# A hybrid decoder layer on one core: the selection of one token block beside the scatter of another

## The chip, the cores and the metric

The kernel runs on one core of one Trainium2 chip. The time is that of one execution on the device, in microseconds (us). A core has five engines with queues of their own: TensorE (PE, with its weight loads shown as PEld), VectorE (DVE), ScalarE (ACT), GpSimd (POOL) and SyncE (SP, which here issues transfers). Each works through its instructions in the order that the program gives, and waits on semaphores for the others.

## The reference

One layer of a causal decoder for 512 tokens of width 1024: latent attention and a convolution beside each other, then a retrieval over experts (PEER), then a gate and a norm. The change lies in the retrieval:

```
q = (xb @ w_q).reshape(P, 8, 2, 64)
s = einsum('phcd,hcnd->phcn', q, sub_keys)            # 8 heads x 2 halves x 128 keys
v1, i1 = top_k(s[:, :, 0], 16); v2, i2 = top_k(s[:, :, 1], 16)
cand = v1[..., :, None] + v2[..., None, :]            # 256 sums for each head
best, pos = top_k(cand, 16)
g = softmax(best)
act = gelu(xb . u_tab[e]);  out = sum over h,k of g * act * v_tab[e]
```

There are 128 x 128 experts; each token picks 8 x 16 of them.

## The kernel before

**Dense and gathered tokens.** The 512 tokens are four blocks of 128. Block 0 gathers its experts' rows from `u_tab` and `v_tab` by indirect transfers (POOL issues them, DVE multiplies: `gu`, `gj`, `gv`, `acc`). Blocks 1 to 3 are computed densely: for each of 128 expert tiles e (128 experts each) `dense_act(e)` multiplies the tile of `u_t` by the 384 tokens in 24 matmuls (`aps`, each fp32 product as three matmuls of split halves, lines 149 to 151) and applies Gelu (`act`); later `dense_out(e)` multiplies by the gates and by the tile of `v_tab` in 18 matmuls (`vps`). Every tile is loaded (`tr`), split into a high half on ACT (`th`, L136) and a low half on DVE (`tl`, L141), two units ahead of its use.

**The early stage.** Before the first `dense_out`, the gates of blocks 1 to 3 must lie in DRAM as a table `gd`. So a first stage runs EARLY = 65 of the tiles' `dense_act` and beside them, on the other engines, the routing. `topk(t)` is called for blocks 0, 1, 2, 3 in turn and has two parts. *Selection*, on DVE: 16 rows of keys (five operations each, two of them with a value load ahead: `tv`, `ti`, `sc`; half of the rows of blocks 0 and 1 lie ahead of this stage), eight heads of candidates (five operations each: `bv`, `bp`, `cand`), softmax and the decoding of the picks (`ge`, `oh`, `sel` and others). For block 0 it ends in `pidx`, with which the gathers can start. *Scatter*, for blocks 1 to 3: three transposes on PE (`str`, L916 to L918) bring picks and gates into another layout, ACT copies them (`ids`, `gsc`), and then 16 groups of eight tokens follow. A group is one comparison on DVE (`o12`, 2048 elements, shown in rows of the trace as `o`), two multiplications by the high and the low part of the gate (`og`, 1024 elements each, L945), 16 matmuls on PE (`gp`, L962 and L963) and two evictions on ACT (`stg`, L964); after two groups SP stores 1 MB to `gd` (L967).

**What sets the order.** The loop over the tiles hands out the routing in small steps: each `yield` in `topk` names its cost on DVE and PE, and steps are taken while the DVE's sum is below a pace times the PE's sum. The kernel's recording layer then schedules: it simulates the engines by its own costs and may move instructions past each other within an engine where nothing depends on them. The gathers of block 0 (18 in this stage) are spread over the tiles from G_FROM on.

**Storage.** Scores (`sc`) of the four blocks share one pool of four buffers with the staging of the scatter (`stg`). Gelu results wait in a ring of RING = 17 buffers; EARLY - RING = 48 of them are spilled to DRAM and loaded back later.

**The end of the stage.** `load_gates` (L1014) reads the first part of `gd` back (`gch`) once the last `stg` has been stored; `prep_out` multiplies it by `act` (`cf`, L1027), splits that (`ch`, `cl`), and the first `vps` can run. After that, `dense_act` and `dense_out` alternate, tile by tile.

Of the kernel before, what the change touches and what calls it, by code (L numbers as in the profile page):

```python
# [46 lines left out]
RING = 17  # L47
# [4 lines left out]
EARLY = 65  # L52
# [6 lines left out]
G_FROM = 20  # L59
EARLY_TOP = (0, 1)  # L60
TOP_PACE = 4
ROUTE_V = 237.0
# [3 lines left out]
A_M = 3.9  # L66
# [28 lines left out]
def hymba_layer(ctx, tc, x, xT, p_t, pos, pvec, conv_ln_g, conv_ln_b, w_in, w_uq, w_ukv, w_out,  # L95
# [52 lines left out]
    def mm3(ps, lh, ll, rh, rl, first, last):  # L148
        nc.tensor.matmul(ps, lh, rh, start=first, stop=False)  # L149
        nc.tensor.matmul(ps, lh, rl, start=False, stop=False)  # L150
        nc.tensor.matmul(ps, ll, rh, start=False, stop=last)  # L151
# [549 lines left out]
    s8p = s8.enter_context(tc.tile_pool(name="s8p", bufs=4, side="right"))  # L701
    sc = [s8p.tile([P, 2 * NH, NK], F32, name=f"sc{t}", tag="s8") for t in range(NT)]
# [7 lines left out]
    with ExitStack() as fs:  # L710
# [3 lines left out]
        def best_keys(t, rs):  # L714
            if t not in tops:
                new_top(t)
            s, (tv, ti) = sc[t], tops[t]
            for r in rs:
                h, c = divmod(r, 2)
                nc.vector.max(out=tv[:, h, c, 0:8], in_=s[:, r])  # L720
                nc.vector.max_index(out=ti[:, h, c, 0:8], in_max=tv[:, h, c, 0:8], in_values=s[:, r])
                nc.vector.match_replace(out=s[:, r], in_to_replace=tv[:, h, c, 0:8], in_values=s[:, r],
                                        imm_value=-3e38)
                nc.vector.max(out=tv[:, h, c, 8:16], in_=s[:, r])
                nc.vector.max_index(out=ti[:, h, c, 8:16], in_max=tv[:, h, c, 8:16], in_values=s[:, r])
                yield 1.0, 0.0
# [42 lines left out]
    ready = {}  # L769

# [13 lines left out]
    def dense_act(e):  # L784
        hi, lo = ready.pop(("A", e))
        ps = ps_a.tile([P, TD], F32, name="aps", tag="a")
        for k in range(KD):
            mm3(ps, hi[:, k], lo[:, k], xnh[:, k, P:], xnl[:, k, P:], k == 0, k == KD - 1)
# [31 lines left out]
    with ExitStack() as fs:  # L820
# [14 lines left out]
        def topk(t):  # L835
# [12 lines left out]
            for h in range(NH):  # L848
# [6 lines left out]
                yield (1.9 if h == 0 else 0.8), 0.0  # L855
# [37 lines left out]
            for j0, w in ((0, 8), (8, 16)):  # L893
# [6 lines left out]
                yield (1.2 if w == 16 else 0.7) + (1.8 if j0 == 0 else 0.0), 0.0  # L900
# [3 lines left out]
                yield (1.2 if w == 16 else 0.7), 0.0  # L904
# [5 lines left out]
                yield (0.9 if j0 == 0 else 1.4), 0.0  # L910
            if t == 0:
                nc.vector.scalar_tensor_tensor(pidx, sel[:, 0], float(NK), sel[:, 1], op0=ALU.mult, op1=ALU.add)
                return
# [3 lines left out]
            nc.tensor.transpose(pt[:, 1], sel[:, 1], identf)  # L917
            nc.tensor.transpose(pt[:, 2], pg, identf)  # L918
            ids = ohp.tile([P, P // PAIR, 2, PAIR], F16, name="ids", tag="ids")
            nc.scalar.activation(ids, pt[:, 0:2].rearrange("p c (g q) -> p g c q", q=PAIR), AF.Copy)  # L920
            gh = ohp.tile([P, P], F16, name="gh", tag="gh")
            gl = ohp.tile([P, P], F16, name="gl", tag="gl")
            gs = ohp.tile([P, P], F32, name="gsc", tag="gsc")
            nc.scalar.activation(gs, pt[:, 2], AF.Copy, scale=GSC)
            nc.vector.tensor_copy(gh, gs)
            nc.vector.tensor_tensor(gl, gs, gh, op=ALU.subtract)
            yield 1.2, 0.3

            late = []
            for c in range(P // TCH):  # L930
                stg = s8p.tile([P, NK, TCH], F32, name="stg", tag="s8")
                for c0 in range(0, TCH, OCH):
                    cs = slice(c * TCH + c0, c * TCH + c0 + OCH)
                    ng = OCH // PAIR
                    gs0 = cs.start // PAIR
                    o12 = ohp.tile([P, ng, 2, NK, PAIR], F16, name="o12", tag="o12")
                    og = ohp.tile([P, 2, ng, NK, PAIR], F16, name="og", tag="og")
# [3 lines left out]
                        ids[:, gs0:gs0 + ng].rearrange("p g c q -> p (g c) q").unsqueeze(2)  # L941
                        .to_broadcast([P, 2 * ng, NK, PAIR]), op=ALU.is_equal)
                    yield 1.2, 0.0
# [5 lines left out]
                    o1 = o12[:, :, 0]  # L949
                    late.append((c, c0, stg, o1, og))  # L950
                    if len(late) > LATE:
                        scatter(t, *late.pop(0))
                    yield 1.1, 0.94
# [3 lines left out]
        def scatter(t, c, c0, stg, o1, og):  # L957
            for q in range(0, OCH, 4):
                gp = ps_g.tile([P, 4, NK], F32, name="gp", tag="gp")
                for i in range(4):  # L960
                    g, r = divmod(q + i, PAIR)
                    nc.tensor.matmul(gp[:, i], o1[:, g, :, r], og[:, 0, g, :, r], start=True, stop=False)  # L962
                    nc.tensor.matmul(gp[:, i], o1[:, g, :, r], og[:, 1, g, :, r], start=False, stop=True)  # L963
# [4 lines left out]

        def route():
            for t in (0, 1, 2, 3):  # L970
                yield from topk(t)
# [7 lines left out]
        for e in range(EARLY):  # L979
# [5 lines left out]
            while ngat < want:  # L985
# [3 lines left out]
            while vec < pace * mat:  # L989
                v, m = next(rt, (1e9, 0.0))  # L990
                vec += v
                mat += m
        for _ in rt:
            pass
# [255 lines left out]
```

## Time and profile before

| | us |
|---|---|
| median of 3 runs | 1554.48 (1546.46 to 1557.81) |
| profiled execution, its own time | 1550.69 |
| its span, first to last instruction | 1548.7 |
| PE busy | 1490.1 (96%) |
| DVE busy | 1263.9 (82%) |
| ACT busy | 715.5 (46%) |

The mean granted clock of TensorE is 0.99 of its full level. A matmul's duration overlaps that of the next one, so the busy time of PE is read together with counts: how many matmuls end in a stretch. The same holds on DVE, where the next instruction starts a little before the end of the one ahead; so costs are taken from start to start. The stage that the change touches lies between the first `aps` at 331.8 us and the first `vps` at 684.6 us of the span.

### The profile page before, as it was taken

The page shows a single profiled execution, that of the slowest core. Times are in us where ns is not written, and L with a number is a line of the kernel's source. Part 1 is how long each engine was busy: PE and PEld are TensorE (multiplying, and loading weights), DVE is VectorE, ACT ScalarE, POOL GpSimd, SP SyncE. Part 2 cuts the span into 40 slices and gives each one's busy share as a digit, 9 for nine tenths or more (in the row PEclk, how much of TensorE's full clock was granted, in tenths as well). Part 3 has the DMA queues.
Part 4 walks back from the last instruction along what each step waited for, and adds up shares of the span by engine and source line. Part 5 has one row for each costly group of instructions (what it writes and reads, how often), then busy time and mean ns, then how long its engine had stood idle before and what let it go on. Part 6 is the DMA issues. An engine that isn't in the chain of part 4 may idle for free.

```text
span 1548.7 us, 22818 instructions
## 1 busy us (share of the span) xinstructions
PE 1490.1 (96%) x8070; PEld 1314.2 (85%) x8070; DVE 1263.9 (82%) x2614; ACT 715.5 (46%) x1160; POOL 414.6 (27%) x302
## 2 busy tenths in 40 slices
PE   8999989999899998999999999999999999999997
PEld 6888878799798998899999898888999888878876
DVE  6999665699999999968868777697978788778766
ACT  7468864444484753843333323232333343333444
POOL 0000010001001010014545454364545345435000
PEclk9999989999999999999999999999999999999999
DMA  7321124526587775799999898889999999999642
GB/s 229 103 83 55 49 76 162 177 79 207 170 304 228 260 271 198 269 328 351 336 316 333 304 342 307 307 318 329 341 325 340 336 336 344 342 353 315 225 141 95
DMA packets 167682, 386.55 MB, mean 250 GB/s; under 512 B 13328, under 2 KB 82320, under 8 KB 164496
## 3 DMA queue, kind: packets, MB, share of 16 engines
q1 hardware_dynamic: 130128, 249.82, 47.2%
q0 software_dynamic: 36864, 134.23, 24.1%
q8 instruction: 63, 1.03, 0.3%
q10 hardware_dynamic: 576, 1.05, 0.2%
q14 instruction: 51, 0.42, 0.1%
HBM read 343.63 MB, written 41.42 MB: 249 GB/s over the span
## 4 chain that ended last, share of the span: by engine, by line
DMA 20%; issue 15%; PE 10%; DVE 6%; POOL 5%; ACT 2%; SPq 0%; POOLq 0%; DVEq 0%; ACTq 0%
DMA gu<-in_u_tab,pidx 8%; DMA gv<-in_v_tab,pidx 7%; PE vps L150 3%; PE vps L151 3%; PE vps L149 3%; DMA tr<-in_v_tab 3%; POOL gv L814 3%; POOL gu L803 2%; DMA tr<-in_u_t 1%; DVE tl L141 1%; DVE gj L807 1%; DVE acc L817 1%; DVE cf L1027 1%; ACT th L136 1%; DVE cl L141 1%
## 5 line engine op out<-in xcount | busy, mean ns | idle before, releaser
L136 ACT ACTIVATE th<-tr 128x1024 fp32r<-128x1024 f32 x256 | 270.8, 1059 | 554.9 <-DMA tr<-in_u_t 269.2
L141 DVE SCALAR_TENSOR_TENSOR tl<-tr,th 128x1024 fp32r<-128x1024 f32 x256 | 312.1, 1219 | 119.4 <-ACT th L136 118.9
L149 PE MATMUL aps<-mixh,th 128*128 128x384 f32 x1024 | 348.8, 341 | 4.4 <-ACT act L790 4.4
L151 PE MATMUL aps<-mixh,tl 128*128 128x384 f32 x1024 | 347.5, 339 | 1.1 <-DVE tl L141 1.0
L150 PE MATMUL aps<-mixl,th 128*128 128x384 f32 x1024 | 346.7, 339 | 0.0
L803 POOL DMA_INDIRECT gu<-in_u_tab,pidx x128 | 176.6, 1380 | 533.9 <-DVE gj L807 357.7
L150 PE MATMUL vps<-tl,ch 128*128 128x512 f32 x768 | 301.1, 392 | 7.3 <-DVE tl L141 7.3
L149 PE MATMUL vps<-th,ch 128*128 128x512 f32 x768 | 299.2, 390 | 1.7 <-ACT th L136 1.7
L151 PE MATMUL vps<-th,cl 128*128 128x512 f32 x768 | 299.9, 391 | 0.0
L814 POOL DMA_INDIRECT gv<-in_v_tab,pidx x128 | 211.5, 1653 | 237.0 <-DVE acc L817 201.1
L149 PEld LDWEIGHTS aps<-mixh,th 128*128 128x128 f32 x1024 | 193.9, 189 | 9.0 <-ACT act L790 6.7
L151 PEld LDWEIGHTS aps<-mixh,tl 128*128 128x128 f32 x1024 | 193.8, 189 | 2.7 <-DVE tl L141 2.7
L150 PEld LDWEIGHTS aps<-mixl,th 128*128 128x128 f32 x1024 | 194.0, 189 | 2.3
L807 DVE SCALAR_TENSOR_TENSOR gj<-gu,xn 128x1024 bf16<-128x1024 f32 x128 | 156.1, 1220 | 33.2 <-DMA gu<-in_u_tab,pidx 32.1
L150 PEld LDWEIGHTS vps<-tl,ch 128*128 128x128 f32 x768 | 144.1, 188 | 40.3 <-DVE tl L141 11.8
L817 DVE SCALAR_TENSOR_TENSOR acc<-gv,gact,acc 128x1024 f32<-128x1024 f32 x128 | 163.8, 1279 | 16.8 <-DMA gv<-in_v_tab,pidx 16.0
L149 PEld LDWEIGHTS vps<-th,ch 128*128 128x128 f32 x768 | 144.2, 188 | 31.1 <-ACT th L136 2.5
L151 PEld LDWEIGHTS vps<-th,cl 128*128 128x128 f32 x768 | 144.1, 188 | 29.8
L964 ACT ACTIVATE stg<-gp 128x512 f32<-128x512 f32 x96 | 94.8, 1110 | 21.4 <-PE gp L963 13.7
L136 ACT ACTIVATE ch<-cf 128x384 fp32r<-128x384 f32 x128 | 66.2, 519 | 72.4 <-DVE cf L1027 45.0
L138 ACT ACTIVATE wh<-wr,pv 128x512 fp32r<-128x512 f32 (+2 forms) x84 | 55.1, 694 | 53.2 <-PE bank L151 25.8
L141 DVE SCALAR_TENSOR_TENSOR cl<-cf,ch 128x384 fp32r<-128x384 f32 x128 | 70.5, 551 | 8.2 <-ACT ch L136 8.2
(301 smaller groups left out, 2178.1 us busy)
## 6 DMA issues: line engine op xcount, KB each, us to landing
tr<-in_u_t SPq DMA_DIRECT2D x128, 512.0 KB, 5.7
tr<-in_v_tab SPq DMA_DIRECT2D x128, 512.0 KB, 6.8
gd<-stg SPq DMA_DIRECT2D x24, 1024.0 KB, 4.9
gch<-gd SPq DMA_DIRECT2D x64, 384.0 KB, 10.2
ad<-act SPq DMA_DIRECT2D x48, 192.0 KB, 4.0
aback<-ad SPq DMA_DIRECT2D x48, 192.0 KB, 6.8
wr<-in_gate_w SPq DMA_DIRECT2D x12, 512.0 KB, 3.3
wr<-in_w_out SPq DMA_DIRECT2D x8, 512.0 KB, 3.3
```

The costliest lines, as they stand in the source:

```text
L136: nc.scalar.activation(hi, src, AF.Copy)
L138: nc.scalar.activation(hi, src, AF.Copy, scale=g)
L141: nc.vector.scalar_tensor_tensor(lo, src, 1.0 if g is None else g, hi.bitcast(F32), op0=ALU.mult, op1=ALU.subtract)
L149: nc.tensor.matmul(ps, lh, rh, start=first, stop=False)
L150: nc.tensor.matmul(ps, lh, rl, start=False, stop=False)
L151: nc.tensor.matmul(ps, ll, rh, start=False, stop=last)
L803: nc.gpsimd.indirect_dma_start(out=g, out_offset=None, in_=u_tab, in_offset=bass.IndirectOffsetOnAxis(ap=pidx[:, s:s + 1], axis=0))
L807: nc.vector.scalar_tensor_tensor(junk, g, 1.0, xn0, op0=ALU.mult, op1=ALU.mult, accum_out=gact[:, s:s + 1]))
L814: nc.gpsimd.indirect_dma_start(out=g, out_offset=None, in_=v_tab, in_offset=bass.IndirectOffsetOnAxis(ap=pidx[:, s:s + 1], axis=0))
L817: nc.vector.scalar_tensor_tensor(acc0, g, gact[:, s:s + 1], acc0, op0=ALU.mult, op1=ALU.add))
L964: nc.scalar.activation(stg[:, :, c0 + q:c0 + q + 4].rearrange("p n t -> p t n"), gp, AF.Copy, scale=1.0 / GSC)
L1027: nc.vector.tensor_tensor(cf.rearrange("p (c t) -> p c t", t=TCH), a.rearrange("p (c t) -> p c t", t=TCH), gch[c][:, :, e % GCH], op=ALU.mult)
```

## The change

1. *Selection and scatter become separate functions.* `topk(t)` is split into `select(t)` and `gates(t, slots)`. The order of the blocks was selection 0, selection and scatter 1, selection and scatter 2, selection and scatter 3. It becomes: selection 1; the scatter of 1 beside selection 0 and then selection 2; the scatter of 2 beside selection 3; the scatter of 3. `side_by_side` deals the steps of two generators in proportion.
2. *The transposes wait for tiles.* `gates` yields nothing until two further expert tiles have been handed out, then issues its three transposes behind the last matmul of the newest tile (`issue_after`), and splits the gates on DVE one tile later.
3. *One multiplication for a group's gates.* High and low part of the gate lie in one tile `ghl`; the group's two multiplications of 1024 elements become one of 2048, with four free dimensions.
4. *Storage and numbers.* Each score block has a buffer of its own, and a scatter stages in the buffers that are free by then. RING is 18, EARLY 66 (so 48 tiles are spilled as before), the 18 early gathers begin at tile 41 instead of 21 and not before `pidx` is there, and the costs in the `yield`s and of the pace are new.

```diff
-RING = 17
+RING = 18
-EARLY = 65
+EARLY = 66
-G_FROM = 20
+G_FROM = 40
-ROUTE_V = 237.0
+ROUTE_V = 255.0
-A_M = 3.9
+A_M = 4.16
...
+        def tiles_later(n):
+
+            e = last_tile[0] + n
+            while last_tile[0] < e:
+                yield None
+
+        def gates(t, slots):
+            yield from tiles_later(2)
+            sel, pg = chosen.pop(t)
 
             pt = ps_tr.tile([P, 4, P], F32, name="str", tag="tr")
-            nc.tensor.transpose(pt[:, 0], sel[:, 0], identf)
...
+            with tc.issue_after(last_tile[1]):
+                nc.tensor.transpose(pt[:, 0], sel[:, 0], identf)
+                nc.tensor.transpose(pt[:, 1], sel[:, 1], identf)
+                nc.tensor.transpose(pt[:, 2], pg, identf)
...
-                    for part, gate in ((0, gh), (1, gl)):
-                        nc.vector.tensor_tensor(
-                            og[:, part], o12[:, :, 1],
-                            gate[:, cs].rearrange("p (g q) -> p g q", q=PAIR).unsqueeze(2)
-                            .to_broadcast([P, ng, NK, PAIR]), op=ALU.mult)
...
+                    nc.vector.tensor_tensor(
+                        og, o12[:, :, 1].unsqueeze(2).to_broadcast([P, ng, 2, NK, PAIR]),
+                        ghl[:, g0:g0 + ng].unsqueeze(3).to_broadcast([P, ng, 2, NK, PAIR]), op=ALU.mult)
...
+        def side_by_side(a, b, va, vb):
+
+            da = db = 0.0
+            while a is not None or b is not None:
+                w = None
+                if a is not None and (b is None or db / vb > 0.1 + da / (0.85 * va)):
+                    try:
+                        w = next(a)
+                    except StopIteration:
+                        a = None
+                        continue
+                    da += w[0] if w else 0.0
+                if w is None and b is not None:
...
+                yield w
...
         def route():
-            for t in (0, 1, 2, 3):
-                yield from topk(t)
+            yield from select(1)
+            yield from side_by_side(gates(1, (1, 0)), chain(select(0), select(2)), 36.0, 75.0)
+            yield from side_by_side(gates(2, (1, 0, 2)), select(3), 36.0, 43.0)
+            yield from gates(3, (1, 0, 2, 3))
```

**VectorE, second half of the scatter of block 1.** Before, the groups follow each other with hardly anything between them (`sc_3293` are the scores of block 2):

```order
L938 TENSOR_TENSOR o_4946<-iok,ids 128x2048
L141 SCALAR_TENSOR_TENSOR tl<-tr,th 128x1024
L945 TENSOR_TENSOR og<-o_4946,gh 128x1024
L945 TENSOR_TENSOR og<-o_4946,gl 128x1024
L938 TENSOR_TENSOR o_4973<-iok,ids 128x2048
L725 MAX_INDEX ti_5276<-tv_5275,sc_3293 128x8
L945 TENSOR_TENSOR og<-o_4973,gh 128x1024
L945 TENSOR_TENSOR og<-o_4973,gl 128x1024
```

Now the key rows of block 3 (`sc_3294`) stand between them; this piece holds one of the groups:

```order
L141 SCALAR_TENSOR_TENSOR tl<-tr,th 128x1024
L954 TENSOR_TENSOR o_5498<-iok,ids 128x2048
L725 MAX_INDEX ti_5902<-tv_5901,sc_3294 128x8
L961 TENSOR_TENSOR og<-o_5498,ghl 128x2048
L721 MAX_INDEX ti_5902<-tv_5901,sc_3294 128x8
L720 MAX tv_5901<-sc_3294 128x8
L722 MATCH_REPLACE sc_3294<-tv_5901,sc_3294 128x128
L721 MAX_INDEX ti_5902<-tv_5901,sc_3294 128x8
L724 MAX tv_5901<-sc_3294 128x8
L722 MATCH_REPLACE sc_3294<-tv_5901,sc_3294 128x128
```

From the ninth group of block 1 to its sixteenth, the selection of block 3 has moved in between, though the program text hands it out beside the scatter of block 2.

**ScalarE, from the last evictions (`stg`) to the first split of the gated products (`ch`).** Before:

```order
L964 ACTIVATE stg<-gp 128x4x128 x2
L136 ACTIVATE th<-tr 128x1024
L790 ACTIVATE act<-aps 128x384
L136 ACTIVATE th<-tr 128x1024
L790 ACTIVATE act<-aps 128x384
L136 ACTIVATE th<-tr 128x1024
L790 ACTIVATE act<-aps 128x384
L136 ACTIVATE ch<-cf 128x384 x2
```

Now:

```order
L792 ACTIVATE act<-aps 128x384
L136 ACTIVATE th<-tr 128x1024
L978 ACTIVATE stg<-gp 128x4x128 x4
L136 ACTIVATE th<-tr 128x1024 x2
L136 ACTIVATE ch<-cf 128x384
L792 ACTIVATE act<-aps 128x384
L136 ACTIVATE ch<-cf 128x384
```

Three Gelus (`act`) of expert tiles stood between the last eviction and the first `ch`; now none does. On TensorE the same shows in counts: between the last matmul of the scatter and the first `vps` stood 118 `aps` matmuls (22 of one tile and four whole tiles), now 38 (14 of one tile and one whole tile).

## Rows read from the trace of the kernel before

**Rows 1.** The page, part 1: busy time of each engine.

```profile
PE 1490.1 (96%) x8070; PEld 1314.2 (85%) x8070; DVE 1263.9 (82%) x2614; ACT 715.5 (46%) x1160; POOL 414.6 (27%) x302
```

**Rows 2.** Busy time by stretch: start:end, us, PE, PEld, DVE, ACT, POOL (instructions), clock, DMA.

```profile
331.82:684.60 352.78, 338.01 (x2390) 322.33 (x2388) 335.88 (x1027) 202.22 (x254) 25.21 (x23) 0.98 0.69 236
331.88:663.06 331.18, 316.41 (x2255) 300.89 (x2255) 326.55 (x1014) 192.04 (x240) 24.05 (x21) 0.98 0.67 232
```

**Rows 3.** Waits of TensorE, 331.8 to 684.6: total us, times, longest.

```profile
PE str L916 <- DVE sel L909: 8.8, 3, 3.6
```

**Rows 4.** Waits of ScalarE and VectorE, same stretch and columns.

```profile
ACT ids L920 <- PE str L918: 8.3, 3, 4.4
...
DVE tl L141 <- ACT th L136: 13.3, 7, 2.9
```

**Rows 5.** TensorE in order of time at the second set of transposes: start, us, row.

```profile
502.91 0.33 PE L916 MATMUL str<-identf,sel 128*128 128x128 f32 x1 [3.64 <-DVE sel L909]
```

**Rows 6.** Busy time by stretch, as Rows 2: first tile, six tiles, scatter, half clock.

```profile
331.82:335.28 3.46, 3.46 (x30) 3.29 (x28) 3.46 (x25) 2.78 (x6) 0.00 (x0) 1.00 0.45 152
465.82:490.78 24.96, 24.96 (x145) 24.96 (x145) 24.93 (x126) 11.54 (x15) 1.87 (x2) 1.00 0.73 227
513.21:515.03 1.82, 1.82 (x33) 1.82 (x33) 1.77 (x7) 1.80 (x3) 0.94 (x1) 1.00 0.39 158
503.40:506.80 3.40, 3.40 (x13) 3.40 (x12) 3.40 (x12) 0.56 (x2) 0.00 (x0) 0.50 0.79 282
```

**Rows 7.** VectorE in order of time, beside the scatter of block 3.

```profile
652.36 0.68 DVE L945 TENSOR_TENSOR og<-o,gh 128x1024 f16<-128x1024 f16 x1
652.96 0.69 DVE L945 TENSOR_TENSOR og<-o,gl 128x1024 f16<-128x1024 f16 x1
653.56 1.22 DVE L938 TENSOR_TENSOR o<-iok,ids 128x2048 f16<-128x2048 f16 x1
654.70 1.22 DVE L807 SCALAR_TENSOR_TENSOR gj<-gu,xn 128x1024 bf16<-128x1024 f32 x1
655.84 0.08 DVE L807 DVE_READ_ACCUMULATOR gj<-gu,xn 128x1 f32 x1
```

**Rows 8.** VectorE in order of time: ten key operations, a split; eleven candidate operations.

```profile
367.62 0.46 DVE L720 MAX8 tv<-sc 128x8 f32<-128x128 f32 x2
...
369.96 1.21 DVE L141 SCALAR_TENSOR_TENSOR tl<-tr,th 128x1024 fp32r<-128x1024 f32 x1
371.08 0.48 DVE L720 MAX8 tv<-sc 128x8 f32<-128x128 f32 x2
...
380.48 0.08 DVE L854 MATCH_VALUE_LOAD bp<-bv,cand 128x8 f32 x1
...
382.54 0.22 DVE L853 MAX8 bv<-cand 128x8 f32<-128x80 f32 x1
```

**Rows 9.** VectorE groups, 331.88 to 663.06: busy, mean ns, idle before.

```profile
L141 DVE SCALAR_TENSOR_TENSOR tl<-tr,th 128x1024 fp32r<-128x1024 f32 x60 | 73.3, 1221 | 4.0 <-ACT th L136 3.8
L807 DVE SCALAR_TENSOR_TENSOR gj<-gu,xn 128x1024 bf16<-128x1024 f32 x17 | 20.6, 1212 | 0.0
```

**Rows 10.** TensorE in order of time: going on after the last scatter.

```profile
664.05 0.42 PE L151 MATMUL aps<-mixh,tl 128*128 128x384 f32 x1
664.32 0.34 PE L149 MATMUL aps<-mixh,th 128*128 128x384 f32 x1
```

**Rows 11.** All engines in order of time: from the last eviction to the second products.

```profile
666.63 0.33 SPq L967 DMA_DIRECT2D gd<-stg  x1
673.25 4.07 SPq L1014 DMA_DIRECT2D gch<-gd  x5
...
681.13 1.03 DVE L1027 TENSOR_TENSOR cf<-act,gch 128x384 f32<-128x384 f32 x2 [2.51 <-DMA gch<-gd]
682.41 0.56 DVE L141 SCALAR_TENSOR_TENSOR cl<-cf,ch 128x384 fp32r<-128x384 f32 x1 [0.25 <-ACT ch L136]
...
684.60 0.39 PE L149 MATMUL vps<-th,ch 128*128 128x512 f32 x1
```

More of the change, by code (lines that the diff above doesn't have):

```diff
@@ L150, in mm3 @@
         nc.tensor.matmul(ps, lh, rl, start=False, stop=False)
-        nc.tensor.matmul(ps, ll, rh, start=False, stop=last)
+        return nc.tensor.matmul(ps, ll, rh, start=False, stop=last)
     mixp = ctx.enter_context(tc.tile_pool(name="mixp", bufs=1))
@@ L700, in hymba_layer @@
     s8 = ExitStack()
-    s8p = s8.enter_context(tc.tile_pool(name="s8p", bufs=4, side="right"))
-    sc = [s8p.tile([P, 2 * NH, NK], F32, name=f"sc{t}", tag="s8") for t in range(NT)]
+    s8p = s8.enter_context(tc.tile_pool(name="s8p", bufs=1, side="right"))
+    sc = [s8p.tile([P, 2 * NH, NK], F32, name=f"sc{t}", tag=f"s8{t}") for t in range(NT)]
     tops = {}
@@ L903, in topk @@
                                             tib[:, :w, c].unsqueeze(2).to_broadcast([P, w, 8, NH]), op=ALU.mult)
[L904 removed]
+                yield (1.2 if w == 16 else 0.8), 0.0
                 while w > 2:
@@ L927, in topk @@
-            yield 1.2, 0.3
+            ghl = ohp.tile([P, P // PAIR, 2, PAIR], F16, name="ghl", tag="ghl")
+            gs = ohp.tile([P, P // PAIR, PAIR], F32, name="gsc", tag="gsc")
+            nc.scalar.activation(gs, pt[:, 2].rearrange("p (g q) -> p g q", q=PAIR), AF.Copy, scale=GSC)
+            yield from tiles_later(1)
+            nc.vector.tensor_copy(ghl[:, :, 0], gs)
+            nc.vector.tensor_tensor(ghl[:, :, 1], gs, ghl[:, :, 0], op=ALU.subtract)
+            yield 0.5, 0.3
             late = []
@@ L967, in scatter, with chain @@
                 nc.sync.dma_start(gd[(t - 1) * (P // TCH) + c], stg)
+        def side_by_side(a, b, va, vb):
[10 more added lines that the diff above has]
+                if w is None and b is not None:
+                    try:
+                        w = next(b)
+                    except StopIteration:
+                        b = None
+                        continue
+                    db += w[0]
+                yield w
+        def chain(*gs):
+            for g in gs:
+                yield from g
         def route():
-            for t in (0, 1, 2, 3):
-                yield from topk(t)
+            yield from select(1)
+            yield from side_by_side(gates(1, (1, 0)), chain(select(0), select(2)), 36.0, 75.0)
+            yield from side_by_side(gates(2, (1, 0, 2)), select(3), 36.0, 43.0)
+            yield from gates(3, (1, 0, 2, 3))
         rt, gu = route(), gathered()
@@ L984, in hymba_layer @@
             want = (e + 1 - G_FROM) * G_EARLY / (EARLY - G_FROM)
-            while ngat < want:
+            while placed and ngat < want:
                 next(gu, None)
@@ L989, in hymba_layer @@
             while vec < pace * mat:
[L990 to L994, printed above, removed]
+                w = next(rt, (1e9, 0.0))
+                if w is None:
+                    break
+                vec += w[0]
+                mat += w[1]
+        for w in rt:
+            assert w is not None
     s8.close()
```

49 lines of the change are left out of this document (22 added, 27 removed).

## The prediction

> **What bounds the kernel now.** I read the page first. TensorE is busy 96% of the span and VectorE 82% [rows 1], so at most some 58 us are left to be had from TensorE in the whole kernel. Then the table of stretches: the stage that the change touches takes 352.78 us, TensorE busy 338.01 and VectorE 335.88 of them [rows 2]. Both are nearly full, so neither alone explains it, and the count decides: how long would TensorE need for what it does there? A tile of 24 `aps` matmuls takes 24.96 / 6 = 4.16 us, a matmul 0.173; 32 scatter matmuls take 1.82, so a group of 16 takes 0.91; the first matmul and the last 26 of the scores before it take 3.46 [rows 6]. The first `aps` matmul after a scatter takes 0.27 from start to start and not 0.17 [rows 10], so each return costs 0.10. The order before has 1584 `aps` matmuls, 48 groups, 76 returns and nine transposes (0.11 each, from 0.33 for three: an `aps` follows at 503.24 the first transpose at 502.91 [rows 5]) in the stage: 3.46 + 1583 x 0.1733 + 48 x 0.91 + 76 x 0.10 + 1.0 = 330 us. It takes 352.8, so 23 us are lost. The waits say where: TensorE waits three times for the end of a selection, 8.8 us [rows 3], the second time 3.64 us [rows 5]; after it the clock is granted at 0.50 for 3.4 us [rows 6], which is the 1.2 of its two levels, 1.2 and 2.4 GHz. Then ScalarE waits for the transposes, 8.3 us [rows 4], and VectorE, whose next work needs `ids`, stands behind it. A round trip at each of three blocks: this is what the change goes for.
>
> **The change, part by part.**
>
> *The round trips.* In the new order, 39 and 59 tiles stand ahead of the second and third transposes, and the selections that they need end on VectorE well before. Those waits go. Not all 23 us come back: the stage then ends by the longer of the two engines' work, and by what follows.
>
> *VectorE's total.* It is busy 326.55 us from the start of the stage to its last `og` [rows 2]. The two multiplications go from start to start in 0.60 each, the comparison of 2048 elements in 1.14 [rows 7]. No row has a multiplication of 2048. It could cost from 1.14 (as the comparison) up to 2.28, twice the 1.14 of a 1024-element fp32 operation that stands beside it [rows 7], if it lost the rate of 16-bit data. Below 1.14 nothing points. I take 1.14, since type, element count and innermost pair are those of the comparison. That saves 0.06 x 48 = 2.9 us. Three more weight splits stand ahead of the last `og` (63, not 60 [rows 9]), at 1.12 to 1.14: +3.4. VectorE's total stays at 327. The Trainium skill, "VectorE: DVE Perf Modes", section "Side-by-side: where the cycles go for N=2048 bf16", counts about 150 cycles of set-up for each instruction; by that, an estimate from the page, one operation instead of two saves 0.17 us and not 0.06, and the sum below would come out 1.7 us lower. The rows show why not: the second multiplication starts 0.60 after the first though each lasts 0.68.
>
> *A new wait in the middle.* The new order on VectorE puts the selection of block 3 between the groups of block 1. Up to the `og` of the fifteenth group it holds 35 splits, 15 comparisons and 15 multiplications, 240 key operations, 139 candidate operations and 103 others. Ten key operations take 2.34 us, eleven candidate operations 2.06, a split 1.12 [rows 8], a gather product 1.14 [rows 7]. The 135 others of the stage get what is left of 326.55: less 60 x 1.13, 48 x 1.14, 96 x 0.60, 17 x 1.14 [rows 9], 240 x 0.234 and 160 x 0.187, that is 41 us or 0.30 each. Sum to that point: 35 x 1.13 + 30 x 1.14 + 240 x 0.234 + 139 x 0.187 + 103 x 0.30 = 39.6 + 34.2 + 56.2 + 26.0 + 31.2 = 187.2 us. TensorE's queue has ahead of that group's matmuls only 871 `aps`, 14 groups, 13 returns and three transposes: 3.46 + 870 x 0.1733 + 14 x 0.91 + 1.3 + 0.3 = 168.6. So TensorE, which takes its queue in order, has waited **18.6 us** by then, whatever else happens; most of it at the eleventh and twelfth groups, which stand next to each other on TensorE with a stretch of selection between them on VectorE. Queued behind it: the tiles 36 and on, and on ScalarE the evictions, behind which the next `th` stand. From there TensorE needs 723 x 0.1733 + 34 x 0.91 + 2.6 + 0.7 = 159.5 us to the end of the last group, VectorE only 327 - 187 = 140, so TensorE sets the rest.
>
> *The end of the stage.* Before, TensorE went on after the last scatter matmul at 664.05 [rows 10]; the last store was issued at 666.63, the read-back at 673.25, the gated product began at 681.13 and its split ended at 682.41 + 0.56 = 682.97 [rows 11]. That chain, **18.9 us**, was hidden: 118 `aps` matmuls lay behind the last scatter, and the first `vps` followed at 684.60 without a wait [rows 11]. Now 38 lie there, 6.6 us. So 12.3 us of the chain are bare. After such a pause the clock: 3.4 us at half [rows 6] lose 1.7.
>
> *The rest.* RING, EARLY and the spill move with each other; a tile done earlier is a tile less later. The early gathers start later, but their products (17 before the last `og`, as before) fall where VectorE has 20 us of room. If that room went, each would delay TensorE by 1.14.
>
> *The sum.* First `vps` after 187.2 + 159.5 + 18.9 = 365.6 us of the stage, with 68 tiles done. Before: 352.8 with 66; two more at 4.16 make 361.1. Difference +4.5, with the clock +6.2. Against the profiled execution of 1550.69 that is 1556.9. The median of the runs stands 3.8 above that execution, so I forecast a median of **1560 us**: the round trips go, and a wait in the middle and a bare chain at the end take their place. Its own range is 1553 to 1568, from 3 us either way on the two engines' sums and a few of scatter between runs.
>
> **The rivals.**
>
> *A. The wait in the middle does not come*, because the key and candidate operations next to scatter groups run tighter than my prices or the fifteenth group is not that late: 365.6 - 18.6 = 347.0, so -14.1 + 1.7: about 1542. Against it: the sum of prices is tied to VectorE's own busy time. Chance 0.14.
>
> *B. It goes as the change is meant*, neither the middle nor the end bare: 12.3 and the clock's 1.7 less again, about 1528. It needs a chain under 7 us, where 14.5 of the 18.9 are transfers [rows 11]. Chance 0.08.
>
> *C. Slower by ScalarE's queue.* Six evictions (groups 11 to 13) now stand in one piece ahead of the next `th`, and VectorE's `tl` waits for that `th`, with `og` of the next groups behind it: the loop closes over three engines, just where TensorE is already late. The longest such wait before was 2.9 us, 13.3 in seven [rows 4]; four of them there would add 12 to the middle wait: 1572. It decides if `th` comes over a tile late at groups 11 to 15. Chance 0.15.
>
> *D. Slower by the multiplication with four free dimensions*, which is then not "one operation for two" in time: at 2.28 us, VectorE gets 48 x 1.14 = 54.7 us more, the last `og` comes at 382, and the first `vps` at 382 + 0.9 + 18.9 = 401.6: +40.5, 1595. It takes the lead from some 1.55 us an operation on (VectorE's 20 us of room, over 48). Against it: the comparison has as many repeated elements and runs at 1.14. Chance 0.09.
>
> **How the numbers follow.** Forecast 0.54, A 0.14, B 0.08, C 0.15, D 0.09. The range 1541 to 1573 takes in the forecast, most of A and most of C; B, D and the edges of A and C, some 0.2, lie outside. A change under 1% (15.5 us: 1539 to 1570) can hardly be told from none with three runs. Faster than that: B and a fifth of A, 0.11. Slower: D, half of C, the edge of the forecast, 0.18. The rest, 0.71, is within.
>
> **What would show it.** In the profile after: no wait of TensorE on the end of a selection, and ScalarE's wait for the transposes gone or harmless; in their place waits of scatter matmuls on `og`, together 15 to 20 us, around 36 tiles into the stage; a pause of TensorE of about 12 us before the first `vps` with VectorE waiting for the read-back of the gates; `og` with 2048 elements at about 1.22 us duration. No wait on `og` in the middle means A; a first `vps` right behind an `aps` means the chain was shorter, B; long waits of `tl` for `th` near group 12 mean C; `og` over 1.6 us means D. I would be wrong altogether if the time after the stage changed: its 801 us hold the same work.

## The result, and the profile after

The change takes **1563.88 us** (median of 20 runs, 1548.94 to 1571.58) against 1552.95 for the kernel before in the same rounds: ratio **1.0066 [1.0047, 1.0085]**. In another set of rounds (after_again, below) it gave 1561.95, ratio 1.0046 [1.0022, 1.0070]. It is slower by about half a per cent, 7 to 10 us; the forecast was 1560, 6 us slower.

The page shows little of it. Busy times of the whole execution, against [rows 1]:

```profile
PE 1493.6 (95%) x8070; PEld 1323.6 (85%) x8070; DVE 1261.9 (81%) x2566; ACT 714.1 (46%) x1160; POOL 423.8 (27%) x302
```

VectorE has 48 instructions fewer and 2 us less to do; TensorE is busy for 3.5 us more with the same matmuls, since more of them ran at the lower clock (its mean granted clock is 0.98 and was 0.99). The stage tells more. The table of stretches of the change: the whole stage, up to the last scatter, the pause on ScalarE's account, the stretch at half clock at the end, the first output tile. Columns: start:end, length, busy time of PE, PEld, DVE, ACT, POOL with instruction counts, granted clock, DMA share, GB/s.

```profile
332.73:700.46 367.73, 341.33 (x2437) 332.53 (x2436) 335.76 (x979) 204.83 (x258) 33.30 (x22) 0.97 0.67 228
332.73:681.20 348.47, 334.54 (x2400) 326.06 (x2398) 328.74 (x970) 197.43 (x250) 31.62 (x21) 0.98 0.66 226
385.50:395.30 9.80, 5.09 (x18) 4.77 (x18) 9.77 (x46) 4.36 (x6) 0.00 (x0) 0.65 0.27 95
692.30:705.90 13.60, 5.44 (x13) 4.28 (x14) 8.94 (x15) 4.20 (x7) 2.29 (x3) 0.50 1.14 329
700.46:707.22 6.76, 6.76 (x19) 5.34 (x19) 6.76 (x13) 1.64 (x4) 3.04 (x3) 0.60 1.09 361
```

The stage takes 367.7 us with 68 tiles in it. Before, it took 352.8 with 66 [rows 2], which is 361.1 at 68. So 6.6 us of the loss lie here. The waits of that stretch (total us, times, longest) answer to [rows 3] and [rows 4]:

```profile
ACT ge L863 <- DVE ge L862: 15.9, 3, 8.3
PE vps L149 <- ACT ch L136: 12.5, 1, 12.5
PE gp L976 <- DVE og L961: 9.0, 2, 8.8
DVE tl L141 <- ACT th L136: 21.6, 10, 8.5
PE aps L149 <- ACT act L792: 4.7, 1, 4.7
```

No wait of TensorE on `sel` is left and none of ScalarE on the transposes: the round trips are gone. Three other waits of TensorE, 26.2 us, stand in their place. The first is the new one in the middle. TensorE and VectorE in order of time there (start, us, row, idle before and what ended it):

```profile
497.59 1.20 DVE L961 TENSOR_TENSOR og<-o,ghl 128x2048 f16<-128x2048 f16 x1
507.77 1.22 DVE L961 TENSOR_TENSOR og<-o,ghl 128x2048 f16<-128x2048 f16 x1
514.29 2.35 DVE L961 TENSOR_TENSOR og<-o,ghl 128x2048 f16<-128x2048 f16 x2
518.73 1.21 DVE L961 TENSOR_TENSOR og<-o,ghl 128x2048 f16<-128x2048 f16 x1
```

```profile
509.05 0.29 PE L976 MATMUL gp<-og,o 128*128 128x128 f16 x1 [8.83 <-DVE og L961]
```

Ten us lie between two gate multiplications that TensorE needs one right after the other, and VectorE is not idle in them: it does two splits, a comparison and, for the rest of the time, key and candidate operations of block 3's selection. The last `og` row is the fifteenth multiplication; it ends some 1.14 later, at 519.87, which is **187.1 us** into the stage. The forecast was 187.2. In that whole stretch VectorE (third busy time) stands idle for 0.6 us only, so its own queue sets this point:

```profile
332.73:519.87 187.14, 173.60 (x1126) 170.60 (x1124) 186.55 (x776) 89.15 (x117) 5.80 (x4) 0.95 0.56 184
```

The second is the end of the stage, which answers to [rows 11]. SyncE's issues, VectorE, and TensorE:

```profile
685.93 0.32 SPq L981 DMA_DIRECT2D gd<-stg  x1
690.86 5.48 SPq L1057 DMA_DIRECT2D gch<-gd  x6
```

```profile
699.17 1.03 DVE L1070 TENSOR_TENSOR cf<-act,gch 128x384 f32<-128x384 f32 x2 [3.32 <-DMA gch<-gd]
```

```profile
681.13 0.22 PE L977 MATMUL gp<-og,o 128*128 128x128 f16 x1
700.46 0.79 PE L149 MATMUL vps<-th,ch 128*128 128x512 f32 x1 [12.46 <-ACT ch L136]
```

From the end of the last scatter matmul (0.06 after 681.13) to the first `vps` it takes 19.3 us, and TensorE stands idle for 12.5 of them. Then the clock is at its lower level: 0.50 up to 705.9, so that the first output tile takes 6.76 us; 18 matmuls at the 0.23 from start to start that they have later would be 4.1.

The third wait nobody had foreseen. ScalarE in order of time:

```profile
379.34 1.28 ACT L863 ACT_TABLE_LOAD   x1
388.89 0.31 ACT L863 ACTIVATE ge<-ge 128x128 f32<-128x128 f32 x1 [8.27 <-DVE ge L862]
389.22 1.28 ACT L792 ACT_TABLE_LOAD   x1
390.51 0.49 ACT L792 ACTIVATE act<-aps 128x384 f32<-128x384 f32 x1
```

The exponential of block 0's selection stands in ScalarE's queue ahead of a tile's Gelu. It waits 8.3 us for VectorE, and the Gelu behind it, and with it the accumulator that TensorE wants next. TensorE pauses for 4.7 us, up to 391.05, and runs at half clock up to 395.3 (the clock had been low from 388.5 on, in the pause): 4.9 us lost by the pause with the slow start behind it, and half of the 4.2 at the low clock, 7.0 in all.

### The profile page after: what moved, and what is told of

The parts are those of the page before. It is cut to its first block, busy times and chain, and to the rows that moved or that the text cites. A ratio compares the mean times of both kernels' runs of the same rounds, so it can differ in the third digit from the quotient of the medians.

```text
span 1564.0 us, 22763 instructions
## 1 busy us (share of the span) xinstructions
PE 1493.6 (95%) x8070; PEld 1323.6 (85%) x8070; DVE 1261.9 (81%) x2566; ACT 714.1 (46%) x1160; POOL 423.8 (27%) x302
## 4 chain that ended last, share of the span: by engine, by line
PE 31%; DVE 22%; DMA 19%; issue 17%; ACT 5%; POOL 5%; SPq 1%; DVEq 0%; POOLq 0%; ACTq 0%
DMA gu<-in_u_tab,pidx 7%; DMA gv<-in_v_tab,pidx 4%; DMA tr<-in_v_tab 4%; DVE tl L141 3%; PE aps L149 3%; PE aps L150 3%; PE aps L151 3%; PE vps L150 3%; PE vps L151 3%; PE vps L149 3%; POOL gu L805 3%; DVE o L954 2%; DVE cacc L305 2%; PE bank L150 2%; PE bank L151 2%
## 5 line engine op out<-in xcount | busy, mean ns | idle before, releaser
L805 POOL DMA_INDIRECT gu<-in_u_tab,pidx x128 | 181.4, 1417 | 541.7 <-DVE gj L809 373.5
L149 PE MATMUL vps<-th,ch 128*128 128x512 f32 x768 | 300.4, 391 | 14.8 <-ACT ch L136 12.5
L816 POOL DMA_INDIRECT gv<-in_v_tab,pidx x128 | 215.9, 1687 | 234.1 <-DVE acc L819 200.6
L149 PEld LDWEIGHTS aps<-mixh,th 128*128 128x128 f32 x1024 | 194.2, 190 | 12.1 <-ACT act L792 9.8
L819 DVE SCALAR_TENSOR_TENSOR acc<-gv,gact,acc 128x1024 f32<-128x1024 f32 x128 | 163.9, 1281 | 20.5 <-DMA gv<-in_v_tab,pidx 19.3
```

The lines of the kernel that those rows point to most:

```text
L805: nc.gpsimd.indirect_dma_start(out=g, out_offset=None, in_=u_tab, in_offset=bass.IndirectOffsetOnAxis(ap=pidx[:, s:s + 1], axis=0))
L816: nc.gpsimd.indirect_dma_start(out=g, out_offset=None, in_=v_tab, in_offset=bass.IndirectOffsetOnAxis(ap=pidx[:, s:s + 1], axis=0))
L819: nc.vector.scalar_tensor_tensor(acc0, g, gact[:, s:s + 1], acc0, op0=ALU.mult, op1=ALU.add))
```

## The experiments

Each ran in rounds shared with the kernel before, whose median in them was 1552.5 to 1554.1. "Stage" is from the first `aps` to the first `vps` in one profile; "at 68" adds 4.16 us for each tile short of 68. The two kernels that were profiled twice (the change and after_again, hold270_exps and best_again) differ from themselves by 0.9 and 2.2 us of stage, so differences of 1 or 2 us in that column tell nothing.

| kernel | median us | ratio to before | stage (tiles) | at 68 |
|---|---|---|---|---|
| before | 1553 | 1 | 352.8 (66) | 361.1 |
| the change | 1563.9 | 1.0066 [1.0047, 1.0085] | 367.7 (68) | 367.7 |
| after_again | 1562.0 | 1.0046 [1.0022, 1.0070] | 366.9 (68) | 366.9 |
| hold | 1556.8 | 1.0002 [0.9975, 1.0029] | 362.1 (68) | 362.1 |
| rv270 | 1550.7 | 0.9968 [0.9946, 0.9990] | 354.3 (67) | 358.4 |
| hold270 | 1552.8 | 0.9979 [0.9948, 1.0011] | 352.8 (67) | 356.9 |
| split | 1564.0 | 1.0074 [1.0049, 1.0100] | 371.9 (68) | 371.9 |
| exp_late | 1559.4 | 1.0057 [1.0034, 1.0079] | 367.5 (68) | 367.5 |
| no_lag | 1557.1 | 1.0025 [1.0004, 1.0045] | 366.0 (68) | 366.0 |
| only_merge | 1550.6 | 0.9991 [0.9977, 1.0006] | 349.6 (66) | 357.9 |
| hold270_exp | 1551.4 | 1.0007 [0.9985, 1.0028] | 355.3 (67) | 359.5 |
| rv270_exps | 1552.9 | 0.9987 [0.9963, 1.0011] | 353.3 (67) | 357.5 |
| hold270_exps | 1545.4 | 0.9934 [0.9905, 0.9963] | 351.2 (67) | 355.3 |
| best_again | 1549.0 | 0.9968 [0.9945, 0.9992] | 349.0 (67) | 353.2 |

The theory: two losses took the place of the round trips, VectorE's queue ahead of the fifteenth group, and the chain behind the last scatter. The rivals: that the waits were only signs of TensorE's own lateness, or one lag counted twice.

### Take away the middle wait: hold

The key rows of block 3 may start on VectorE only behind the last gate multiplication of block 1.

```
 def best_keys(t, ...):
-    nc.vector.max(out=tv[:, h, c, 0:8], in_=s[:, r])
+    with tc.issue_after(behind[t]) if t in behind else nullcontext():
+        nc.vector.max(out=tv[:, h, c, 0:8], in_=s[:, r])
...
 def gates(t, slots):
...
-            nc.vector.tensor_tensor(og, ...)
+            last_og = nc.vector.tensor_tensor(og, ...)
...
+    if t == 1:
+        behind[3] = last_og.ins
```

> The change with one thing undone in the middle: on VectorE the selection of block 3 may start only behind the last gate multiplication of block 1, so it no longer stands between groups 9 to 16 of that block. Theory (the middle wait is VectorE's work ahead of the fifteenth group, 18.6 us): the sum of prices ahead of that group falls from 187 to some 163 us, under TensorE's 168.6; the 8.8 us wait of scatter matmuls on the multiplication and the lag spread over the tiles around it go; 68 tiles still stand ahead of the first output matmul and 38 matmuls behind the last scatter, so the bare chain at the end (12 us and the half clock) stays. First vps about 350 us into the stage, not 367.7: about 18 us less than the change, 1546, ratio to before about 0.995. Rival 1: the time lost around the middle is TensorE's own (more returns, slower matmuls beside the scatter) and the wait only a symptom: it comes back elsewhere, 1560 to 1565. Rival 2: the other selection work held back now delays the third block's groups: a wait of transposes on sel or of scatter on the multiplication in block 3, more than 8 us, time 1555 to 1565.

Measured: 1556.8, about 7 us less than the change, 5.6 of them in the stage; 18 were expected, and the time lies where rival 2 put it. The middle wait itself is gone. TensorE's waits in the stage:

```profile
PE vps L149 <- ACT ch L136: 12.3, 1, 12.3
PE aps L149 <- ACT act L794: 4.9, 2, 4.7
PE gp L980 <- DVE og L963: 4.5, 1, 4.5
```

The one of 4.5 is new, in block 2's scatter at 275 us of the stage, where the selection that was held back now stands on VectorE: rival 2's mechanism, at half its size. The other part of the shortfall is the 4.7 on ScalarE with the half clock behind it. The change has it too, but there it lay ahead of the point that VectorE's 187 us set, and cost nothing. Here the fifteenth multiplication ends at 175.5, and VectorE is busy for 165.2 of them:

```profile
332.81:508.28 175.47, 170.66 (x1125) 167.44 (x1123) 165.15 (x614) 89.19 (x117) 5.79 (x4) 0.99 0.61 196
```

TensorE's queue, with the forecast's 168.6, 4.9 for that pause and 1.7 for the 3.4 us at half clock behind it, gives 175.2, and is now the later of the two. So the verdict is that the wait was real and worth what lies between it and the **next** bound, not its own length.

### Cover the chain at the end: rv270, and both: hold270

`ROUTE_V` is VectorE's work for the routing, in the pace of the loop over the tiles. With a larger number the routing is handed out sooner; in the trace the last scatter comes four tiles earlier.

```
-ROUTE_V = 255.0
+ROUTE_V = 270.0
```

> The change with one number changed, the planned vector work (255 to 270), so that the groups are spread over fewer tiles and the last scatter is four tiles earlier: 110 aps matmuls (19 us) stand behind it, as 118 did in the kernel before. Theory (the chain from the last scatter to the first output matmul, 19 us, was bare for 12.3 us and cost some 1.5 to 2.7 more in half clock): the 12.5 us wait of vps on ch goes or falls under 2; the middle wait stays as it is or grows by a few us since the groups come sooner. About 12 to 14 us less than the change: 1550 to 1552, ratio to before about 0.999. Rival: the middle lag grows by as much as the end gains (TensorE reaches group 11 two tiles earlier, 8 us, with VectorE at the same place): the time stays within 4 us of the change, 1560 to 1568, with the wait of scatter on the multiplication up from 8.8 to 17 us or so.

Measured: 1550.7, 13 less than the change, as the theory said; its stage is 9.3 shorter at 68 tiles, about what the last pause lost (12.5 to 2.9). With 110 `aps` matmuls behind the last scatter the pause before the first `vps` is 2.9:

```profile
PE gp L976 <- DVE og L961: 7.6, 4, 4.4
PE aps L149 <- ACT act L792: 6.6, 2, 4.8
PE vps L149 <- ACT ch L136: 2.9, 1, 2.9
```

It is not 0 since the chain grew, from 19.3 to 22.2 us: the read-back, issued at 673.29, lets `cf` start only at 686.58, 13.3 us later, where in the change it was 8.3 (690.86 to 699.17) with TensorE idle. The running tiles alone don't explain that, since before, with TensorE running all through it, the same step took 7.9 (673.25 to 681.13 [rows 11]). What slowed it stays open.

> Both edits: selection of block 3 held behind the last multiplication of block 1, and the planned vector work at 270. Theory: middle wait and bare chain are two separate losses, one in VectorE's queue, one behind the last scatter, and both go: first vps about 336 us into the stage with 67 tiles (about 340 at 68), 27 to 30 us less than the change, 1534 to 1537, and faster than the kernel before by 1.0 to 1.2%, the round trips of its transposes being gone. Rival: they are the same lag, counted twice (TensorE late in the middle is late at the end): the gain of both together is that of one, 12 to 18 us, 1546 to 1552.

Measured: 1552.8, 11 less than the change but no better than rv270; the stage is shorter than rv270's by 1.5. The 27 to 30 us did not come, and the time lies just above the rival's range (1546 to 1552). Whether the two are one lag is not shown by that, though: the middle wait on `og` is down to 2.4 and the last wait to 2.6, as planned. What is left is ScalarE, 9.3 us in four:

```profile
PE aps L149 <- ACT act L794: 9.3, 4, 4.7
PE vps L149 <- ACT ch L136: 2.6, 1, 2.6
PE gp L980 <- DVE og L963: 2.4, 2, 1.3
```

### The stall on ScalarE: exp_late, hold270_exp

On ScalarE the exponential is put behind a Gelu that the loop gave out shortly before. Exp_late does this in the change, for block 0's exponential alone; hold270_exp does it on top of hold270.

```
-nc.scalar.activation(ge, ge, AF.Exp)
+with tc.issue_after(last_gelu[-3]) if t == 0 else nullcontext():
+    nc.scalar.activation(ge, ge, AF.Exp)
```

> The change with one thing moved on ScalarE alone: the exponential of block 0's selection, which stood ahead of the Gelu of tile 10 and held it for 8.3 us (TensorE: 4.9 us of pause, then 6.8 us at half clock, 8.3 us in all), is put behind the Gelu of the 13th tile; TensorE's and VectorE's orders stay but for the two operations that use the exponential. Theory (at the fifteenth group TensorE's delay was bounded by VectorE's 187 us of work, and this stall of 8.3 lies ahead of that point and was hidden in it): the pause at 386 goes, the wait of scatter matmuls on the gate multiplication grows by as much, from 9.0 to about 17 us, and the time stays: 1561 to 1565. Rival: pauses add up, and 7 to 8 us come back: 1555 to 1557.

Measured: the pause at 386 us is gone and tile 20 starts at 89.5 us of the stage, not at 96.0. And the stage is as long as it was, 367.5 against 367.7. The fifteenth multiplication ends at 187.0, in the change at 187.1. This is the plainest proof of the middle bound: 6.5 us saved ahead of it vanish. (The expectation's 8.3 counted half clock that lay inside the pause.) One detail was wrong: the wait on `og` did not grow from 9.0 to 17. It fell to 6.6, and two waits for ScalarE came ahead of it. The longer, of 3.9, stands behind the exponential of block 2, which waits 8.4 us in the same way; now TensorE is early enough to notice. The time, 1559.4, is 3 to 5 us under the change's two medians, within the intervals, and between the two forecasts; the stage decides here, and not the time. TensorE's waits and that of the exponentials in exp_late's stage:

```profile
ACT ge L865 <- DVE ge L863: 11.9, 2, 8.4
PE gp L978 <- DVE og L963: 6.6, 3, 6.2
PE aps L149 <- ACT act L793: 5.3, 2, 3.9
```

> The three edits together: selection of block 3 held behind block 1's last multiplication, planned vector work 270, and the exponential of block 0 behind the Gelu of the 13th tile. Theory: with the hold the middle is no longer bounded by VectorE, so the stall of 8.3 us (4.9 of pause and the half clock behind it), which still stood in the hold270 kernel, is now on the path: the first vps comes at 344 to 346 us of the stage with 67 tiles, not 352.8, and the time is 7 to 8 us below hold270's, 1543 to 1546, faster than the kernel before by 0.5 to 0.7%. Rival: VectorE's sum (336 to the last multiplication and the read-back) bounds the end: less than 3 us come back, 1550 to 1553.

Measured: 1551.4, stage 355.3, nothing gained; the rival's figure again, by another mechanism than the rival's. Block 0's stall is gone; block 2's has come up in its place, longer than before (ScalarE in order of time, then TensorE's waits):

```profile
446.73 1.28 ACT L867 ACT_TABLE_LOAD   x1
457.24 0.31 ACT L867 ACTIVATE ge<-ge 128x128 f32<-128x128 f32 x1 [9.23 <-DVE ge L865]
457.56 1.28 ACT L795 ACT_TABLE_LOAD   x1
```

```profile
PE aps L149 <- ACT act L795: 10.2, 3, 7.4
PE gp L982 <- DVE og L965: 5.4, 5, 1.8
PE vps L149 <- ACT ch L136: 3.0, 1, 3.0
```

### Both exponentials: hold270_exps, rv270_exps

The edit above with `last_gelu[-3 if t == 0 else -2]` for blocks 0 and 2, with the hold and without it.

> The three edits, with a second exponential moved: that of block 2's selection, which stood ahead of the Gelu of tile 24 in hold270_exp and held it for 9.2 us (TensorE: 7.4 of pause, 6.8 us at half clock), now stands behind the Gelu of the 28th tile. Theory: that pause was the surfaced successor of block 0's; with VectorE's sum at 316 us to the last multiplication and nothing of ScalarE in the way, the pause at 119 us of the stage goes and 7 to 11 us come back, less some 3 of small waits on the gate multiplication: first vps at 346 to 349 us of the stage with 67 tiles, time 1543 to 1546, ratio to before 0.994 to 0.997. Rival: a third place takes it up (VectorE is busy 95% of the stage, TensorE 95%; each wait of one is a later wait of the other): stage 353 to 356, 1550 to 1553, ratio 0.999 to 1.001.

Measured: 1545.4, ratio 0.9934 [0.9905, 0.9963], faster than both kernels. Four us of the stage came back, not the 7 to 11 hoped for: at 351.2 it lies between the theory's 346 to 349 and the rival's 353 to 356. TensorE's waits are now all small:

```profile
PE gp L982 <- DVE og L965: 4.7, 3, 2.8
PE gp L982 <- ACT stg L984: 3.0, 3, 1.7
PE aps L149 <- ACT act L795: 2.9, 3, 1.8
PE vps L149 <- ACT ch L136: 2.8, 1, 2.8
```

> The same two exponentials moved, planned vector work 270, but block 3's selection not held back. Theory: without the hold VectorE's work to the middle groups bounds TensorE again (sum of prices: 9 to 10 us over the held order), so moving the exponentials brings little over the rv270 kernel, whose stage took 354 us with 67 tiles: 351 to 354, time 1547 to 1551, and 3 to 7 us above hold270_exps. Rival: the pauses on ScalarE were the loss in rv270 too, the hold is worth nothing: equal to hold270_exps within 2 us.

Measured: 1552.9, 2 above the range expected, and stage 353.3: moving the exponentials without the hold is worth 0.9 us of the stage. Its wait on `og` has grown to 14.2 from rv270's 7.6: VectorE's queue in the middle takes what ScalarE gave back. The fifteenth multiplication ends at 177.7 us of the stage, in rv270 at 177.3, and VectorE is idle ahead of it for less than half a us in either.

```profile
PE gp L978 <- DVE og L963: 14.2, 6, 4.3
ACT ge L865 <- DVE ge L863: 7.1, 2, 3.6
PE vps L149 <- ACT ch L136: 1.6, 1, 1.6
```

At 68 tiles each of the two edits is worth 1 to 2 us of the stage without the other (the hold 358.4 to 356.9, the exponentials 358.4 to 357.5), and in time nothing (1552.8 and 1552.9 against 1550.7); with both it is 1545.4, and 1549.0 when it ran again (best_again, below). That each covers the other's gain is what the waits above show; how much the pair is worth beyond rv270 is not shown, for best_again's ratio, 0.9968, is that of rv270.

### One part of the change at a time: split, only_merge, no_lag

Split undoes the merged multiplication in the change; only_merge puts it into the kernel before.

```
-nc.vector.tensor_tensor(og, o12[:, :, 1].unsqueeze(2)..., ghl[...].unsqueeze(3)..., op=ALU.mult)
+for z in range(2):
+    nc.vector.tensor_tensor(og[:, :, z], o12[:, :, 1], ghl[:, g0:g0 + ng, z]..., op=ALU.mult)
```

> The change with its third part undone: the gate one-hots as two multiplications of 1024 elements instead of one of 2048. Theory: two go from start to start in 0.60 each and one in 1.14 to 1.16, so VectorE gets 0.05 x 48 = 2 to 3 us more, less than 1 us of it ahead of the fifteenth group: 1564 to 1566, no difference to the change that can be told. Rival by the time of set-up (an operation less is worth 0.17 us or more): 8 us more on VectorE in all and 2.6 ahead of the fifteenth group, 1567 and up. Rival that the four-dimensional operation costs more than two: under 1560.

> The kernel before with the third part of the change alone: one multiplication of 2048 elements in place of two of 1024, nothing of the order of selection and scatter. Theory: 0.05 to 0.06 us for each of 48 on VectorE, 2.4 to 2.9 in all, part of it behind TensorE: 1550 to 1553, no difference to before that can be told. Rival by an operation's set-up (0.17 us each): 5 to 8 us less, 1545 to 1548.

Measured: split 1564.0 and the change 1563.9, no difference in time; its stage is 4.2 longer in the one profile. Only_merge 1550.6, ratio 0.9991 [0.9977, 1.0006], stage 3.2 shorter. In both pairs the part is worth 3 to 4 us of stage at most, and no time that can be told. Split isn't clean at the end: its new order leaves no `aps` matmul behind the last scatter, where the change has 38, so its 4.2 is not the price of the multiplications alone. The groups of the multiplication, in split and in the change (engine, operation, count, shortest, median and longest duration in ns, first and last start):

```profile
L962 DVE TENSOR_TENSOR og<-o,ghl x96: 675/684/702, 407.6 to 686.9; 128x1024 f16<-128x1024 f16 x96
```

```profile
L961 DVE TENSOR_TENSOR og<-o,ghl x48: 1195/1219/1226, 408.8 to 679.0; 128x2048 f16<-128x2048 f16 x48
```

What counts is the time to the next instruction's start: the median of the 96 is 0.602, that of the 48 is 1.135, as for the comparison. Two small ones cost 1.204, so the merged one saves 0.07 each, 3.3 us in all.

> The change without the lag: the transposes are no longer put two tiles behind (no wait for tiles, no fixed place behind a tile's last matmul), the rest as in the change. Theory: the selections run so far ahead now that the second and third transposes find sel done anyhow, and the first one's round trip lies ahead of the fifteenth group, where VectorE's work bounds TensorE: the middle wait and the bare chain stay, 1560 to 1568, like the change. Rival: the lag was what took the round trips away; without it waits of transposes on sel of 3 to 4 us come back at each of three places, ScalarE's copies behind them, 1570 to 1580.

```
 def gates(t, slots):
-    yield from tiles_later(2)
     sel, pg = chosen.pop(t)
...
-    with tc.issue_after(last_tile[1]):
-        nc.tensor.transpose(pt[:, 0], sel[:, 0], identf)
+    nc.tensor.transpose(pt[:, 0], sel[:, 0], identf)
...
-    yield from tiles_later(1)
```

Measured: stage 366.0, no wait on `sel` and none of ScalarE on the transposes, the fifteenth multiplication at 187.1 again. It is the side-by-side order that ends the round trips; the two tiles of lag add nothing to that. Its time, 1557.1, lies below the expected range and some 5 to 7 us under the change with a stage only 1 to 2 shorter; the rest of that difference lies behind the stage and isn't explained.

### Twice the same: after_again, best_again

> The change itself once more, on the chip of this call, for a second profile of the same program. Theory: the stage repeats within 1 us (its length is set by the order of the queues: 367 to 369), while the time behind it, 863.6 us in the first profile, falls in 856 to 866, since the small waits for weight transfers there come and go; the ratio to before 1.005 to 1.008. Rival: the time behind the stage belongs to the program and repeats at 863 to 864, so that the change also costs 4 us or more there.

> The kernel with the three edits and both exponentials moved, once more, on the same chip as the change itself. Theory: stage 350 to 352 us, ratio to before 0.991 to 0.996, some 1.1 to 1.3% under the change. Rival: its gain was the chip's or the day's: ratio 0.997 to 1.001.

Measured, the change: its stage repeats within 0.9 us, the part behind it takes 860.5 where it took 863.6. The stage lies at the lower edge of what was expected and the ratio just below it. The rival, that the rest has a length of its own, is not borne out to 3 us, and single profiles say nothing finer.

Measured, the kernel with all edits: stage 349.0, 1549.0 us, ratio 0.9968 [0.9945, 0.9992]. Only the stage is as good as expected, or better. The gain on the change in the same rounds is 0.8%, not 1.1 to 1.3, and the ratio missed its range and lies at the edge of the rival's. Against the kernel before it is faster in both sets, by 0.3 and by 0.7%: the second gain is half of the first.

## Why the prediction was right

**What the time alone says.** Little: the range of 1541 to 1573 would have held the kernel before as well. What speaks for the prediction is that its terms can be found in the trace, one by one.

**The round trips.** They went, as said, and by the order that the prediction named: no_lag, without the lag of two tiles, has none either. But "VectorE, whose next work needs `ids`, stands behind it" was hardly so: up to its last `og` VectorE was busy for 326.55 of 331.18 us [rows 2]. VectorE's total, which the change leaves as it is, set nearly all of that stretch already; its idle time there, 4.6 us, is the most that better order could have won up to that point.

**VectorE's total.** It was taken as unchanged at 327 to the last multiplication; up to the last scatter VectorE is busy 328.7. The merged operation was taken at 1.14 with 0.06 saved; it measures 1.135 and 0.07. An operation starts before the one ahead of it ends (0.602 from start to start, 0.684 long). The Trainium skill, "VectorE: DVE Perf Modes", section "Side-by-side: where the cycles go for N=2048 bf16", counts about 150 cycles of set-up for each instruction; the prediction's 0.17 was an estimate from that. The trace shows 0.07. It mattered little, as split and only_merge show.

**The middle.** VectorE's 187.2 us to the fifteenth group came out at 187.0 to 187.1 in the change, in exp_late and in no_lag, and at 186.6 in after_again. The sign named for it was off: waits on `og` of 9.0, not 15 to 20. TensorE arrives late by itself, by the 7.0 us that the exponential costs. 168.6 + 7.0 + 9.0, and 2.9 for the half clock from 509.05 to 514.8 behind the wait, make 187.5. A bound at a hand-over says when, not on which wait the time is booked. The prediction had no term for that stall on ScalarE. It was luck that this did no harm: the stall lies ahead of a point that VectorE sets.

**From there to the end.** 161.3 us to the last scatter, forecast 159.5; chain 19.3, forecast 18.9; pause 12.5, forecast 12.3. The half clock costs 2.7 at the first output tile, and was taken as 1.7: the pause of 12.5 left the clock low for longer than the 3.4 us of [rows 6], after a pause of 3.6.

**The sum.** First `vps` at 367.7, forecast 365.6; against before +6.6 in the stage, forecast +4.5; with the clock +9.3, forecast +6.2. The runs say +7 to +10. Counted from 68 tiles on, the time behind the stage is 855.8 in the kernel before (864.1 less 8.3 for two tiles), 863.6 and 860.5 in the change's two profiles, and between 851 and 866 over all the kernels of the table, which share that work. So "its 801 us hold the same work" is neither refuted nor proven finer than that; what moves those us stays open.

**The rivals' prices were wrong, though none of them came.** A and B gave back whole waits: 1542 without the middle wait, 1528 without both. Hold and hold270 took exactly these waits away and gave 1557 and 1553. The step that fails there is "365.6 - 18.6": the next bound lies only some 6 us of stage below, ScalarE's stalls, block 2's scatter and VectorE's total standing close together. C named ScalarE's queue as the danger, and it was one, but through exponentials that wait for VectorE, not through evictions; of the waits of `tl` on `th`, the long one of 8.5 stands in the pause at the end and the nine others, 13.0 together, behind 560 us, none near groups 11 to 15. D is excluded by 1.135 us.

## What to carry to other kernels

Where two engines are both over 90% busy, add up each engine's queue to every hand-over between them and rank the results: the latest tells when the stage ends, and the next one what removing the latest is worth. Price an edit that takes a wait away by that difference, and look for short operations of a third engine (here an exponential with its two table loads) that wait in front of the work that frees a buffer. A chain at a stage's end (store, read-back, first product) wants as much independent work queued behind its start as it lasts. And read a gain from a second set of runs before you state its size.

## What the runs showed of the hardware

- After a pause of TensorE of 3.6 us the granted clock was 0.50 for 3.4 us [rows 6]. In the change it was low for 6.8 us with the pause of 4.7, for 10.2 with that of 8.8, and for 13.7 with that of 12.5, a part of each in the pause itself. What TensorE lost by the low clock once it ran again was 1.7, 2.1, 2.9 and 2.7 us. The pause alone doesn't fix the length: in after_again, with pauses of 4.7, 8.6 and 12.1, it was 6.8, 6.8 and 10.2.
- An exponential between Gelus brought two table loads of 1.28 us on ScalarE. Where it waited for VectorE, as in the change at 379 us, the first of them ran ahead of the wait, and only the second was on the path.
- The same read-back of the gates took 8.3 us with TensorE idle (the change) and, with TensorE running, 7.9 us (before) and 13.3 us (rv270), from its issue to the product that needs it. The cause of the spread is open.
- Two multiplications of 1024 16-bit elements took 1.204 us of VectorE from start to start, and one of 2048 took 1.135.
